# Where the weight blocks of the SwiGLU and projection products stand in SBUF: set in by 116 bytes instead of 112, even chunks ahead of odd ones with 128 bytes between

## The chip, the core and the metric

One core of a Trainium2 chip runs the whole program in one launch. The metric is the device time in microseconds (us). Before the change three runs gave 1672.34, 1673.3 and 1674.23 us; the median is 1673.3. A difference of about 0.2% (3.3 us) is what a measurement of this kernel can tell from no change.

## What is computed

One layer of a decoder, in fp32, for T = 576 tokens (a prompt of 512 and 8 sequences of 8 new tokens) of D = 1024 features:

```
h = modulate(rms_norm(x, n1_g), sh1, sc1)
x = x + 0.5 * g1 * (silu(h @ w1_gate) * (h @ w1_up)) @ w1_down          # D_FF = 2816
h = modulate(rms_norm(x, nm_g), sh2, sc2)
u, v, q, k, rv, rg, ga, gb = split(h @ w_in)                            # 10240 columns
o_a = gelu(u) * chunk_spatial_mix(layer_norm(gelu(v)))
o_b = head_rms(retention(rotary(q), rotary(k), rv)) * silu(rg)
x = x + g2 * (sigmoid(ga) * (o_a @ w_a) + sigmoid(gb) * (o_b @ w_b)) @ w_o
h = modulate(rms_norm(x, n2_g), sh3, sc3)
x = x + 0.5 * g3 * (silu(h @ w2_gate) * (h @ w2_up)) @ w2_down
y = rms_norm(x, final_g)
```

## The kernel before

**Products in three matmuls.** Every large product is made of fp32r matmuls. A weight and an activation are each split into a rounded part and a rest (hi and lo), and a product of 128 features is three matmuls into one PSUM bank: hi x hi, hi x lo, lo x hi. The stationary operand of a matmul is a block of 128x128 weights, the moving one a row of 288 tokens (H, half of T). `prod` (line 640) does this for 512 features, as four chunks of 128 features (j = 0..3), so it is 12 matmuls, all recorded at line 644. `proj` (line 472, matmuls at 478) does the same for the down projections and a few others.

**Two columns of blocks at a time.** FFN 1, FFN 2 and the projections q, k, rg, ga, gb of w_in go through `Plain`, `Pair` and their variants (from line 693 on). A `Pair` takes two blocks of 128 output columns over 1024 features. It makes the two outputs for both token halves by a seven-product scheme (sums of weight blocks such as `S`, `U`, `V` take the place of the eighth product), so it has seven calls of `prod`, 84 matmuls. The first two of each stage are `Plain`, with eight calls.

**The path of a weight.** `block_of` (676) loads one 512x128 block with one DMA on SP's queue into half of a raw tile (`wraw`). `put_hi` (657) rounds it on ACT into a tile `whl` (or, for one block alone, `whs`), `put_lo` (665) takes the rest on DVE into the same tile. ACT and DVE do this for the next pair while PE works on this one.

**Places.** `set_in` (144) makes a tile a little larger than its data and starts the data INTO = 28 words (112 bytes) in. Within a `whl` tile, hi and lo of two blocks follow each other, and each block is its four chunks of 128 words (512 bytes) one after another. The moving operand of chunk j is row j of a tile of [2, 4, 288] words, so these rows are 1152 bytes apart. 1152 is 4.5 times 256 and 512 is twice 256: modulo 256 bytes the distance from a moving row to its weight block moves by 128 from each chunk to the next. A `whl` tile is (2048 + 28) words, 8304 bytes, and the next of its four buffers starts 8320 bytes on, which is 32.5 times 256.

```
 144     def set_in(home, shape, room=INTO, **kw):
 149         t = home.tile([P, n + room], F32R, **kw)[:, INTO:INTO + n]
 642         for j in range(4):
 643             for z, (s, m) in enumerate(((wh, xh), (wh, xl), (wl, xh))):
 644                 PE.matmul(
 645                     ps[:, :H], lhsT=s[:, j * P:(j + 1) * P], rhs=m[:, j, :],
```

**Value products.** In `values_of` (matmuls at 1346 and 1359) and `values` (1576) it is the other way round: tokens are stationary, and 256 columns of a weight tile made by `load_w` move. Those tiles are set in by the same 112 bytes.

**Order.** PE's order is the order in which the code is written; at the three seams between stages it is a list of steps by name (BEGIN, INTO_MIX, INTO_FFN2). In the retention stage (about 750 to 1250 us) work lives in slots of 2304 bytes, of which there are NSLOT = 36, handed out in turn.

Of the kernel before, what the change touches and what calls it, by code (L numbers as in the profile page):

```python
# [8 lines left out]
F32 = mybir.dt.float32  # L9
F32R = mybir.dt.float32r  # L10
AF = mybir.ActivationFunctionType
ALU = mybir.AluOpType
# [3 lines left out]
P = 128  # L16
# [7 lines left out]
H = T // 2  # L24
# [3 lines left out]
DV = 256  # L28
EPS = 1e-6
NT = 5  # L30
SG = 4
NSLOT = 36
NSLOT2 = 12
SSLOT = 11
FSLOT = 12
GROUPS = (5, 6, 5, 6)

INTO = 28
HALF = (slice(0, H), slice(H, T))

BEGIN = """
# [40 lines left out]
def layer_kernel(ctx: ExitStack, tc: tile.TileContext, a):  # L82
    nc = tc.nc
    PE, DVE, ACT, POOL = nc.tensor, nc.vector, nc.scalar, nc.gpsimd
# [5 lines left out]
    wp = ctx.enter_context(tc.tile_pool(name="wp", bufs=1))  # L90
    places = ExitStack()
# [29 lines left out]
    now["sn"], now["whs"] = pool(places, "sn"), pool(places, "whs")  # L121

    def slot(shape, dt=F32):

# [37 lines left out]
    def whl(shape):  # L162
        small = len(shape) == 3 and shape[1] == 1
        tag = "whs" if small else "whl"
        return set_in(now["whs"] if small else wp, [P] + shape, tag=tag, name=nm(tag), bufs=1 if small else 4)
# [8 lines left out]
    def high_low(shape):  # L174
        t = whl([2] + shape)
        return t[:, 0], t[:, 1]

    def split_w(raw, eng=None):
        hi, lo = high_low(list(raw.shape[1:]))
        ACT.copy(out=hi, in_=raw)  # L180
        now["lo"] = (eng or DVE).tensor_tensor(out=lo, in0=raw, in1=hi.bitcast(F32), op=ALU.subtract)  # L181
        return hi, lo

    def load_w(src, k0, kc, c0, cols, eng=None):
        return split_w(load_raw(src, k0, kc, c0, cols), eng)

    def split(hi, lo, src):
        ACT.copy(out=hi, in_=src)  # L188
# [327 lines left out]
    class Operands:  # L516
# [123 lines left out]
    def prod(ps, w, x, fresh):  # L640
        (wh, wl), (xh, xl) = w, x
        for j in range(4):
            for z, (s, m) in enumerate(((wh, xh), (wh, xl), (wl, xh))):
                PE.matmul(  # L644
                    ps[:, :H], lhsT=s[:, j * P:(j + 1) * P], rhs=m[:, j, :],
                    start=fresh and j == 0 and z == 0, stop=j == 3 and z == 2, skip_group_check=True,
                )
        tick(cost(4))

    def snap(ps, t=None):  # L650
# [2 lines left out]
        ACT.copy(out=t, in_=ps[:, :H])  # L653
        return t

    class Weights:
        def put_hi(self, names, src, neg=False):
            hl = whl([2, len(names), 512])
            if neg:
                ACT.activation(out=hl[:, 0], in_=src, func=AF.Copy, scale=-1.0)  # L660
            else:
                ACT.copy(out=hl[:, 0], in_=src)  # L662
            self.hl[names] = hl, src, neg

        def put_lo(self, names):
            hl, src, neg = self.hl[names]
            if neg:
                now["lo"] = DVE.scalar_tensor_tensor(
                    out=hl[:, 1], in0=src, scalar=-1.0, in1=hl[:, 0].bitcast(F32), op0=ALU.mult, op1=ALU.subtract
                )  # L670
            else:
                now["lo"] = DVE.tensor_tensor(out=hl[:, 1], in0=src, in1=hl[:, 0].bitcast(F32), op=ALU.subtract)  # L672
            for i, m in enumerate(names):
                self.w[m] = (hl[:, 0, i], hl[:, 1, i])

        def block_of(self, dst, i, z):
# [16 lines left out]
    class Plain(Weights):  # L693


        def __init__(self, cols, n):
            self.cols, self.n, self.g, self.w, self.hl, self.raw = cols, n, None, {}, {}, []
            for z in range(2):
                t = raw4([2, 4, P])
                for i in range(2):  # L700
                    self.block_of(t[:, i], i, z)
                self.raw.append(t.rearrange("p m k c -> p m (k c)"))

        def nh(self):
            self.put_hi(("n11", "n21"), self.raw[0], True)
# [54 lines left out]
    class Pair(Weights):  # L760
        def __init__(self, cols):
            self.cols, self.w, self.hl = cols, {}, {}
            self.p, self.q = (raw4([2, 4, P]) for _ in range(2))
            for t, m, i, z in ((self.p, 0, 0, 0), (self.q, 1, 1, 0), (self.p, 1, 1, 1), (self.q, 0, 0, 1)):
                self.block_of(t[:, m], i, z)

            self.p, self.q = (t.rearrange("p m k c -> p m (k c)") for t in (self.p, self.q))

        def ah(self):
            self.put_hi(("a11", "a22"), self.p)  # L770
# [2 lines left out]
            self.put_lo(("a11", "a22"))  # L773

        def bh(self):
            self.put_hi(("a12",), self.q[:, 0:1])

        def bl(self):
            self.put_lo(("a12",))

        def S(self):
            DVE.tensor_tensor(out=self.p[:, 1], in0=self.q[:, 1], in1=self.p[:, 1], op=ALU.add)  # L782
            DVE.tensor_tensor(out=self.q[:, 1], in0=self.q[:, 1], in1=self.p[:, 0], op=ALU.add)  # L783

        def U(self):
            DVE.tensor_tensor(out=self.p[:, 0], in0=self.p[:, 1], in1=self.p[:, 0], op=ALU.add)  # L786

        def Sh(self):
            self.put_hi(("s2", "s1"), self.p)
# [2 lines left out]
            self.put_lo(("s2", "s1"))  # L792

        def V(self):
            DVE.tensor_tensor(out=self.q[:, 0], in0=self.p[:, 0], in1=self.q[:, 0], op=ALU.add)

        def Uh(self):
            self.put_hi(("s4", "s3"), self.q)
# [217 lines left out]
    parts = [First(0), First(1)]  # L1016
# [68 lines left out]
    for c in range(KC):  # L1085
# [34 lines left out]
    win = a["w_in"][0]  # L1120
# [433 lines left out]
    v = {}  # L1554
# [3 lines left out]
    I32 = mybir.dt.int32  # L1558

    def weights_v(i, z):  # L1560
        return [load_w(win, 4 * kk, 4, V0 + i * 512 + z * 256, 256) for kk in range(2)]

    def values(i, z, ws):

# [254 lines left out]
    for pr in ([0], [1], [2], [3], [4], [5], [6, 7]):  # L1819
# [4 lines left out]
        for h in range(2):  # L1824
            for c in pr:
                ps = proj(W[c], OA, h)
# [30 lines left out]
    now["xs1"], now["sn"], now["whs"] = pool(ffn2, "xs1"), pool(ffn2, "sn"), pool(ffn2, "whs")  # L1857
    now["wraw"] = pool(ffn2, "raw")
    ops.clear()
    now["hl"] = pool(hreg, "hl", "right")  # L1860
# [185 lines left out]
```

## Time and profile before

| | |
|---|---|
| median of 3 runs | 1673.3 us |
| the profiled execution's own time | 1672.59 us |
| its span, first to last instruction | 1670.8 us |
| PE busy | 1639.0 us, 98% |
| DVE, ACT, POOL busy | 69%, 47%, 17% |
| TensorE's granted clock, share of full speed | 0.997 |
| matmuls of line 644 | 5784 |
| matmuls of line 478 | 4032 |

Instructions on different engines overlap. Matmuls are pipelined, so a single matmul's record (295 ns) is much longer than the time from one matmul's start to the next; the latter is read from the starts and counts of the rows of the timeline. The record of a matmul and the spacing behind it rise and fall together.

### The profile page before, as it was taken

To read this page: it belongs to the slowest core of one execution; us is meant where nothing else is said; L and a number is where in the kernel's file an instruction comes from. 1 tells how busy PE (TensorE), PEld (TensorE's weight loads), DVE (VectorE), ACT (ScalarE), POOL (GpSimd) and SP (SyncE) were. 2 spreads that over 40 slices of the span, in tenths; PEclk is the share of its full clock that TensorE was granted. 3 is DMA by queue.
4 is the path that set the end of the run, shared out by engine and by line. 5 is a ranking of instruction groups with operands and counts; after the bars stand their busy time and mean duration, and the time that the engine had idled before them with its cause. 6 is when DMAs were issued, how large, how long until landed. Compare 5 with 4: busy or idle time off the path is not lost. (4 is left out here: it accounts for less than half of the span.)

```text
span 1670.8 us, 31364 instructions
## 1 busy us (share of the span) xinstructions
PE 1639.0 (98%) x12548; PEld 1576.0 (94%) x12548; DVE 1153.5 (69%) x1835; ACT 783.8 (47%) x1331; POOL 288.1 (17%) x372
## 2 busy tenths in 40 slices
PE   8999999999999999999999999999999999999997
PEld 4889999999999999999989999998999999999997
DVE  6867856576797777755697554676748868576773
ACT  5533524344564556544444454443236525343453
POOL 0000000000411111013245343454231000000002
PEclk9999999999999999999999999999999999999999
DMA  9443444332647676764457575799540333332331
GB/s 306 135 153 109 140 128 137 112 104 86 180 127 221 204 224 197 219 207 149 147 181 226 177 168 157 201 263 266 177 139 8 92 92 96 95 90 81 97 89 58
DMA packets 300212, 252.09 MB, mean 151 GB/s; under 512 B 13593, under 2 KB 260633, under 8 KB 300066
## 3 DMA queue, kind: packets, MB, share of 16 engines
q1 hardware_dynamic: 284594, 206.76, 40.9%
q0 software_dynamic: 13168, 40.97, 8.9%
q10 hardware_dynamic: 2304, 2.36, 0.4%
q8 instruction: 98, 1.61, 0.4%
q14 instruction: 48, 0.39, 0.1%
HBM read 207.01 MB, written 43.02 MB: 150 GB/s over the span
## 5 line engine op out<-in xcount | busy, mean ns | idle before, releaser
L644 PE MATMUL ps<-xa,whl 128*128 128x288 f32 x3000 | 422.4, 295 | 4.4 <-ACT whl L662 1.4
L644 PEld LDWEIGHTS ps<-xa,whl 128*128 128x128 f32 x3000 | 403.4, 190 | 17.3 <-issue 4.2
L644 PE MATMUL ps<-xs,whl 128*128 128x288 f32 x2040 | 289.2, 295 | 0.9 <-ACT sn L653 0.6
L644 PEld LDWEIGHTS ps<-xs,whl 128*128 128x128 f32 x2040 | 274.6, 189 | 11.0 <-issue 4.2
L672 DVE TENSOR_TENSOR whl<-wraw,whl 128x1024 fp32r<-128x1024 f32 x192 | 234.8, 1225 | 56.5 <-ACT whl L662 45.8
L662 ACT CAST whl<-wraw 128x1024 fp32r<-128x1024 f32 x192 | 200.4, 1049 | 111.2 <-DVE wraw L786 65.1
L478 PE MATMUL ps<-c,wd 128*128 128x288 f32 x1824 | 245.8, 295 | 0.0
L478 PEld LDWEIGHTS ps<-c,wd 128*128 128x128 f32 x1824 | 242.4, 188 | 3.5 <-issue 3.4
L478 PE MATMUL ps<-c,whl 128*128 128x288 f32 x1368 | 190.4, 297 | 1.1 <-ACT c L188 0.6
L478 PEld LDWEIGHTS ps<-c,whl 128*128 128x128 f32 x1368 | 182.8, 188 | 3.1 <-ACT c L188 1.1
L465 POOL TENSOR_TENSOR x<-x,s 128x64 f32<-128x64 f32 x72 | 34.8, 484 | 809.7 <-DVE s L464 782.4
L459 DVE SCALAR_TENSOR_TENSOR x<-ps,gate,x 128x288 f32<-128x288 f32 (+1 forms) x128 | 61.1, 481 | 117.2 <-PE ps L478 117.1
L653 ACT COPY sn<-ps 128x288 f32<-128x288 f32 x195 | 77.1, 398 | 104.3 <-PE ps L644 103.7
L181 DVE TENSOR_TENSOR whl<-wraw,whl 128x1024 fp32r<-128x1024 f32 x56 | 75.6, 1351 | 71.2 <-ACT whl L180 70.8
L945 ACT CAST wd<-wraw 128x640 fp32r<-128x640 f32 (+2 forms) x58 | 45.4, 783 | 106.2 <-PE ps L478 100.4
L1346 PE MATMUL ps<-whl,xx 128*128 128x256 f32 x768 | 91.5, 279 | 0.0
L1346 PEld LDWEIGHTS ps<-whl,xx 128*128 128x128 f32 x768 | 90.8, 188 | 0.0
L644 PE MATMUL ps<-xs,whs 128*128 128x288 f32 x480 | 69.7, 293 | 0.0
L180 ACT CAST whl<-wraw 128x1024 fp32r<-128x1024 f32 x56 | 58.5, 1049 | 22.7 <-PE ps L478 14.3
L644 PEld LDWEIGHTS ps<-xs,whs 128*128 128x128 f32 x480 | 65.5, 189 | 0.0
L662 ACT CAST whs<-wraw 128x512 fp32r<-128x512 f32 x62 | 38.4, 620 | 56.4 <-PE ps L644 46.6
L950 DVE TENSOR_TENSOR wd<-wraw,wd 128x640 fp32r<-128x640 f32 (+2 forms) x58 | 53.8, 928 | 9.9 <-ACT wd L945 9.9
(285 smaller groups left out, 2223.4 us busy)
## 6 DMA issues: line engine op xcount, KB each, us to landing
ada<-in_w_ada_dram SPq DMA_DIRECT2D x56, 512.0 KB
wraw<-in_w_in_dram SPq DMA_DIRECT2D x96, 256.0 KB
wraw<-in_w_gate_dram SPq DMA_DIRECT2D x88, 256.0 KB
wraw<-in_w_up_dram SPq DMA_DIRECT2D x88, 256.0 KB
wraw<-in_w_in_dram SPq DMA_DIRECT2D x32, 512.0 KB
wraw<-in_w_down_dram SPq DMA_DIRECT2D x32, 384.0 KB
wraw<-in_w_down_dram SPq DMA_DIRECT2D x32, 320.0 KB
accd<-c POOLq DMA_DIRECT2D x32, 288.0 KB, 5.8
```

The lines of the kernel that those rows point to most:

```text
L180: ACT.copy(out=hi, in_=raw)
L181: now["lo"] = (eng or DVE).tensor_tensor(out=lo, in0=raw, in1=hi.bitcast(F32), op=ALU.subtract)
L459: DVE.scalar_tensor_tensor(out=x[:, o:o + w], in0=ps[:, :w], scalar=g[:, c, 0:1], in1=x[:, o:o + w], op0=ALU.mult, op1=ALU.add)
L465: return lambda: POOL.tensor_tensor(out=x[:, NP:T], in0=x[:, NP:T], in1=u, op=ALU.add)
L478: PE.matmul(ps[:, :H], lhsT=s[:, k, c0:c0 + P], rhs=m[:, HALF[h]], start=k == 0 and z == 0, stop=k == kc - 1 and z == 2,)
L644: PE.matmul(ps[:, :H], lhsT=s[:, j * P:(j + 1) * P], rhs=m[:, j, :], start=fresh and j == 0 and z == 0, stop=j == 3 and z == 2, skip_group ...
L653: ACT.copy(out=t, in_=ps[:, :H])
L662: ACT.copy(out=hl[:, 0], in_=src)
L672: now["lo"] = DVE.tensor_tensor(out=hl[:, 1], in0=src, in1=hl[:, 0].bitcast(F32), op=ALU.subtract)
L945: ACT.copy(out=hl[:, 0], in_=self.raw[c])
L950: DVE.tensor_tensor(out=lo, in0=self.raw[c], in1=hi.bitcast(F32), op=ALU.subtract)
L1346: PE.matmul(ps[:, :DV], lhsT=s, rhs=m, start=i == 0, stop=i == 23)
```

## The change

It does five things.

1. The blocks of `prod` get a layout of their own (`block_w`): in a tile, first the even chunks (0 and 2) of all blocks, hi and then lo, starting BINTO = 29 words (116 bytes) in; then, after 32 free words (128 bytes), the odd chunks (1 and 3) in the same order. So modulo 256 an odd chunk's block stands 128 bytes further than an even chunk's.
2. The raw tiles get the same split, and `block_of` fills a block with two DMAs of 256x128 (even chunks, odd chunks) in place of one of 512x128.
3. ACT's rounding, DVE's rest and DVE's sums of weights read and write two runs in place of one, with the same count of elements and of instructions.
4. Weight tiles of `load_w` for the value products are set in by VINTO = 48 words (192 bytes) in place of 28.
5. A `whl` tile has 64 spare words in place of 28 (8448 bytes, 33 times 256, so that all four buffers start alike modulo 256); `whs` goes ahead of `sn` in memory; NSLOT falls from 36 to 35.

Set side by side by the addresses of the two builds: the distance from a moving row to the block of its own matmul, modulo 256, is 112 and 240 in turn from chunk to chunk before, and 116 in all chunks after. From the moving row to the block that the next matmul needs it is the same number for the first two matmuls of a chunk; for the third, whose next block is that of the next chunk, it is 244 after (before: as the chunk's own). For the value products, from moving row to stationary block, it is 16 or 144 before and 64 after.

```diff
-NSLOT = 36
+NSLOT = 35
 INTO = 28
+VINTO = 48
+BINTO = 29
...
-    def set_in(home, shape, room=INTO, **kw):
+    def set_in(home, shape, room=INTO, into=INTO, **kw):
...
-        t = home.tile([P, n + room], F32R, **kw)[:, INTO:INTO + n]
+        t = home.tile([P, n + room], F32R, **kw)[:, into:into + n]
...
+    def whl(shape, into=INTO):
+        return set_in(wp, [P] + shape, 64, into, tag="whl", name=nm("whl"), bufs=4)
...
-                    ps[:, :H], lhsT=s[:, j * P:(j + 1) * P], rhs=m[:, j, :],
+                    ps[:, :H], lhsT=s[j], rhs=m[:, j, :],
...
+    def block_w(n):
+        half = n * 2 * 2 * P
+        home, tag = (wp, "whl") if n == 2 else (now["whs"], "whs")
+        room = 2 * half + 64
+        t = home.tile([P, room], F32R, tag=tag, name=nm(tag), bufs=4 if n == 2 else 1)
+        parts = []
+        for z in range(2):
+            v = t[:, BINTO + z * n * 256:BINTO + z * n * 256 + 512 * n].rearrange("p (b r) -> p b r", b=2)
+            parts.append(bass.AP(v.tensor, v.offset, [v.ap[0], [half + 32, 2], v.ap[2]]))
+        return parts
...
         def put_hi(self, names, src, neg=False):
-            hl = whl([2, len(names), 512])
+            hl = block_w(len(names))
+            src = src.rearrange("p b m r -> p b (m r)")
...
             for i, m in enumerate(names):
-                self.w[m] = (hl[:, 0, i], hl[:, 1, i])
+                at = [slice(P * (2 * i + j // 2), P * (2 * i + j // 2 + 1)) for j in range(4)]
+                self.w[m] = [[w[:, j % 2, at[j]] for j in range(4)] for w in hl]
...
-            nc.sync.dma_start(
-                out=dst, in_=src[z * 4 * P:(z + 1) * 4 * P, c0:c0 + P].rearrange("(k p) c -> p k c", p=P)
-            )
+            src = src[z * 4 * P:(z + 1) * 4 * P, c0:c0 + P].rearrange("(a b p) c -> p b a c", p=P, b=2)
+            for b in range(2):
+                nc.sync.dma_start(out=t[:, b, m].rearrange("p (a c) -> p a c", c=P), in_=src[:, b])
...
-        wv = [load_w(win, 4 * i, 4, RV0 + hd * DV, DV) for i in range(2)]
+        wv = [load_w(win, 4 * i, 4, RV0 + hd * DV, DV, VINTO) for i in range(2)]
```

PE's and POOL's instructions keep their order and shapes throughout. DVE's and ACT's keep their order too; the subtractions and roundings of blocks have another shape. What is new is on SP's queue. Its opening, where the block loads of FFN 1 (`wraw`) stand between those of the first modulation weights (`xa`, `xs`), before:

```order
L356 DMA xa_165<-in_w_ada_dram 128x2x256 x4
L679 DMA wraw_170<-in_w_gate_dram 128x4x128
L679 DMA wraw_170<-in_w_up_dram 128x4x128
L679 DMA wraw_173<-in_w_gate_dram 128x4x128
L679 DMA wraw_173<-in_w_up_dram 128x4x128
L356 DMA xs_28_176<-in_w_ada_dram 128x2x256 x4
```

and of the change:

```order
L353 DMA xa_165<-in_w_ada_dram 128x2x256 x4
L697 DMA wraw_170<-in_w_gate_dram 128x2x128 x2
L697 DMA wraw_170<-in_w_up_dram 128x2x128 x2
L697 DMA wraw_175<-in_w_gate_dram 128x2x128 x2
L697 DMA wraw_175<-in_w_up_dram 128x2x128 x2
L353 DMA xs_28_180<-in_w_ada_dram 128x2x256 x4
```

Each load of a block has become two of half its size, ahead of the same `xs` loads. Across the program it is 272 block loads that become 544.

## Rows read from the trace of the kernel before

**Rows 1.** The page, part 1: busy time of each engine, its share of the span, instructions.

```profile
PE 1639.0 (98%) x12548; PEld 1576.0 (94%) x12548; DVE 1153.5 (69%) x1835; ACT 783.8 (47%) x1331; POOL 288.1 (17%) x372
```

**Rows 2.** Six stretches of 100 us: length, busy time and instructions of PE, of PE's weight loads, of DVE, ACT and POOL, then the granted clock, the DMA share and GB/s.

```profile
100.00:200.00 100.00, 100.00 (x758) 95.98 (x757) 69.82 (x117) 40.56 (x65) 3.64 (x8) 1.00 0.43 127
300.00:400.00 100.00, 99.77 (x755) 97.30 (x754) 73.33 (x120) 43.41 (x70) 3.09 (x8) 1.00 0.38 111
600.00:700.00 100.00, 100.00 (x757) 93.76 (x754) 76.50 (x114) 62.10 (x104) 10.80 (x20) 1.00 0.70 209
900.00:1000.00 100.00, 100.00 (x824) 97.57 (x824) 56.89 (x76) 45.89 (x82) 38.88 (x43) 1.00 0.60 169
1100.00:1200.00 100.00, 97.90 (x761) 94.33 (x760) 76.94 (x131) 37.94 (x72) 42.55 (x36) 1.00 0.87 259
1500.00:1600.00 100.00, 99.82 (x758) 99.59 (x757) 73.62 (x118) 44.31 (x70) 3.59 (x8) 1.00 0.32 94
```

**Rows 3.** Waits of PE: who waited for whom, us in total, times, longest.

```profile
PE ps L295 <- ACT ada L292: 4.4, 1, 4.4
PE ps L312 <- ACT ada L306: 3.6, 3, 2.0
...
PE ps L644 <- ACT whl L662: 1.4, 1, 1.4
PE ps L644 <- DVE whl L672: 1.3, 2, 0.8
```

**Rows 4.** Groups of PE's matmuls by line and tiles (out<-moving,stationary): count, busy time, mean ns of one record, idle time before them.

```profile
L644 PE MATMUL ps<-xa,whl 128*128 128x288 f32 x3000 | 422.4, 295 | 4.4 <-ACT whl L662 1.4 <-DVE whl L672 1.3 <-ACT xa L557 0.9
L644 PE MATMUL ps<-xs,whl 128*128 128x288 f32 x2040 | 289.2, 295 | 0.9 <-ACT sn L653 0.6
L644 PE MATMUL ps<-xs,whs 128*128 128x288 f32 x480 | 69.7, 293 | 0.0
L644 PE MATMUL ps<-xa,whs 128*128 128x288 f32 x264 | 38.8, 295 | 0.0
...
L1346 PE MATMUL ps<-whl,xx 128*128 128x256 f32 x768 | 91.5, 279 | 0.0
...
L1576 PE MATMUL ps<-whl,xx 128*128 128x256 f32 x384 | 47.9, 282 | 0.0
```

**Rows 5.** PE's timeline in FFN 1, from the end of a down projection (line 478) through two pairs: start, length from first start to last end, line, tiles, count.

```profile
336.86 12.14 PE L478 MATMUL ps<-c,wd 128*128 128x288 f32 x90
348.84 3.31 PE L644 MATMUL ps<-xs,whl 128*128 128x288 f32 x24
351.98 1.74 PE L644 MATMUL ps<-xa,whl 128*128 128x288 f32 x12
353.56 1.74 PE L644 MATMUL ps<-xs,whs 128*128 128x288 f32 x12
355.13 4.89 PE L644 MATMUL ps<-xa,whl 128*128 128x288 f32 x36
359.86 3.32 PE L644 MATMUL ps<-xs,whl 128*128 128x288 f32 x24
363.01 1.74 PE L644 MATMUL ps<-xa,whl 128*128 128x288 f32 x12
364.59 1.74 PE L644 MATMUL ps<-xs,whs 128*128 128x288 f32 x12
366.17 4.89 PE L644 MATMUL ps<-xa,whl 128*128 128x288 f32 x36
370.90 3.31 PE L644 MATMUL ps<-xs,whl 128*128 128x288 f32 x24
374.05 1.74 PE L644 MATMUL ps<-xa,whl 128*128 128x288 f32 x12
```

**Rows 6.** The first of those products at 348.84 us, chunk by chunk: PE's groups in stretches that hold the three matmuls of one chunk and no other, for chunk 0 (349.11 to 349.125 us), chunk 1 (349.50 to 349.52) and chunk 3 (350.29 to 350.305); the row of chunk 2 (349.89 to 349.91) reads as that of chunk 0. The number behind the comma is the mean ns of one record.

```profile
L644 PE MATMUL ps<-xs,whl 128*128 128x288 f32 x3 | 0.6, 295 | 0.0
L644 PE MATMUL ps<-xs,whl 128*128 128x288 f32 x3 | 0.6, 292 | 0.0
L644 PE MATMUL ps<-xs,whl 128*128 128x288 f32 x3 | 0.6, 291 | 0.0
```

**Rows 7.** PE's timeline in the retention stage, around one head's value products (1346, 1359).

```profile
950.39 11.40 PE L1346 MATMUL ps<-whl,xx 128*128 128x256 f32 x96
961.62 2.05 PE L1359 MATMUL ps<-whl,hs 128*128 128x256 f32 x16
963.51 1.76 PE L478 MATMUL ps<-c,whl 128*128 128x288 f32 x12
```

**Rows 8.** DVE's and ACT's groups for the blocks: count, busy time, mean ns of one, idle time before them and what ended it.

```profile
L672 DVE TENSOR_TENSOR whl<-wraw,whl 128x1024 fp32r<-128x1024 f32 x192 | 234.8, 1225 | 56.5 <-ACT whl L662 45.8 <-DMA wraw<-in_w_in_dram 5.2 <-DMA ada<-in_w_ada_dram 1.6
...
L662 ACT CAST whl<-wraw 128x1024 fp32r<-128x1024 f32 x192 | 200.4, 1049 | 111.2 <-DVE wraw L786 65.1 <-PE ps L644 33.7 <-DMA wraw<-in_w_up_dram 7.1
```

**Rows 9.** SP's timeline in the opening (start, length, queue, line, tiles, count) and PE's wait there.

```profile
18.82 0.37 SPq L679 DMA_DIRECT2D wraw<-in_w_gate_dram  x1
19.57 0.37 SPq L679 DMA_DIRECT2D wraw<-in_w_up_dram  x1
20.31 0.81 SPq L679 DMA_DIRECT2D wraw<-in_w_gate_dram  x1
21.16 1.28 SPq L679 DMA_DIRECT2D wraw<-in_w_up_dram  x1
22.48 5.58 SPq L356 DMA_DIRECT2D xs<-in_w_ada_dram  x8
...
31.32 4.07 PE L300 MATMUL ps<-xs,cs 128*32 128x512 f32 x10 [0.34 <-DMA xs<-in_w_ada_dram]
```

More of the change, by code (lines that the diff above doesn't have):

```diff
@@ L120, in layer_kernel @@
     now["xa"], now["xs1"] = pool(places, "xa"), pool(places, "xs1")
-    now["sn"], now["whs"] = pool(places, "sn"), pool(places, "whs")
+    now["whs"], now["sn"] = pool(places, "whs"), pool(places, "sn")
     def slot(shape, dt=F32):
@@ L160, in raw4 @@
         )
[L162 to L165, printed above, removed]
+    def whl(shape, into=INTO):
+        return set_in(wp, [P] + shape, 64, into, tag="whl", name=nm("whl"), bufs=4)
     def load_raw(src, k0, kc, c0, cols):
@@ L172, in load_raw, with split_w, load_w @@
         return raw
[L174 to L179, printed above, removed]
+    def split_w(raw, into=INTO):
+        t = whl([2] + list(raw.shape[1:]), into)
+        hi, lo = t[:, 0], t[:, 1]
         ACT.copy(out=hi, in_=raw)
-        now["lo"] = (eng or DVE).tensor_tensor(out=lo, in0=raw, in1=hi.bitcast(F32), op=ALU.subtract)
+        now["lo"] = DVE.tensor_tensor(out=lo, in0=raw, in1=hi.bitcast(F32), op=ALU.subtract)
         return hi, lo
-    def load_w(src, k0, kc, c0, cols, eng=None):
-        return split_w(load_raw(src, k0, kc, c0, cols), eng)
+    def load_w(src, k0, kc, c0, cols, into=INTO):
+        return split_w(load_raw(src, k0, kc, c0, cols), into)
     def split(hi, lo, src):
@@ L654, in snap, with blocks @@
         return t
+    def block_w(n):
[8 more added lines that the diff above has]
+        return parts
     class Weights:
+        def blocks(self):
+            return raw4([2, 2, 2, P]).rearrange("p b m a c -> p b m (a c)")
         def put_hi(self, names, src, neg=False):
-            hl = whl([2, len(names), 512])
+            hl = block_w(len(names))
+            src = src.rearrange("p b m r -> p b (m r)")
             if neg:
-                ACT.activation(out=hl[:, 0], in_=src, func=AF.Copy, scale=-1.0)
+                ACT.activation(out=hl[0], in_=src, func=AF.Copy, scale=-1.0)
             else:
-                ACT.copy(out=hl[:, 0], in_=src)
+                ACT.copy(out=hl[0], in_=src)
             self.hl[names] = hl, src, neg
@@ L668, in put_lo, with block_of @@
                 now["lo"] = DVE.scalar_tensor_tensor(
-                    out=hl[:, 1], in0=src, scalar=-1.0, in1=hl[:, 0].bitcast(F32), op0=ALU.mult, op1=ALU.subtract
+                    out=hl[1], in0=src, scalar=-1.0, in1=hl[0].bitcast(F32), op0=ALU.mult, op1=ALU.subtract
                 )
             else:
-                now["lo"] = DVE.tensor_tensor(out=hl[:, 1], in0=src, in1=hl[:, 0].bitcast(F32), op=ALU.subtract)
+                now["lo"] = DVE.tensor_tensor(out=hl[1], in0=src, in1=hl[0].bitcast(F32), op=ALU.subtract)
             for i, m in enumerate(names):
-                self.w[m] = (hl[:, 0, i], hl[:, 1, i])
-        def block_of(self, dst, i, z):
+                at = [slice(P * (2 * i + j // 2), P * (2 * i + j // 2 + 1)) for j in range(4)]
+                self.w[m] = [[w[:, j % 2, at[j]] for j in range(4)] for w in hl]
+        def block_of(self, t, m, i, z):
             src, c0 = self.cols[i]
-            nc.sync.dma_start(
-                out=dst, in_=src[z * 4 * P:(z + 1) * 4 * P, c0:c0 + P].rearrange("(k p) c -> p k c", p=P)
-            )
+            src = src[z * 4 * P:(z + 1) * 4 * P, c0:c0 + P].rearrange("(a b p) c -> p b a c", p=P, b=2)
+            for b in range(2):
+                nc.sync.dma_start(out=t[:, b, m].rearrange("p (a c) -> p a c", c=P), in_=src[:, b])
         def finish_hi(self):
@@ L698, in __init__ @@
             for z in range(2):
-                t = raw4([2, 4, P])
+                t = self.blocks()
                 for i in range(2):
-                    self.block_of(t[:, i], i, z)
-                self.raw.append(t.rearrange("p m k c -> p m (k c)"))
+                    self.block_of(t, i, i, z)
+                self.raw.append(t)
         def nh(self):
@@ L762, in __init__ @@
             self.cols, self.w, self.hl = cols, {}, {}
-            self.p, self.q = (raw4([2, 4, P]) for _ in range(2))
+            self.p, self.q = self.blocks(), self.blocks()
             for t, m, i, z in ((self.p, 0, 0, 0), (self.q, 1, 1, 0), (self.p, 1, 1, 1), (self.q, 0, 0, 1)):
-                self.block_of(t[:, m], i, z)
-            self.p, self.q = (t.rearrange("p m k c -> p m (k c)") for t in (self.p, self.q))
+                self.block_of(t, m, i, z)
         def ah(self):
@@ L775, in bh @@
         def bh(self):
-            self.put_hi(("a12",), self.q[:, 0:1])
+            self.put_hi(("a12",), self.q[:, :, 0:1])
         def bl(self):
@@ L781, in S @@
         def S(self):
-            DVE.tensor_tensor(out=self.p[:, 1], in0=self.q[:, 1], in1=self.p[:, 1], op=ALU.add)
-            DVE.tensor_tensor(out=self.q[:, 1], in0=self.q[:, 1], in1=self.p[:, 0], op=ALU.add)
+            DVE.tensor_tensor(out=self.p[:, :, 1], in0=self.q[:, :, 1], in1=self.p[:, :, 1], op=ALU.add)
+            DVE.tensor_tensor(out=self.q[:, :, 1], in0=self.q[:, :, 1], in1=self.p[:, :, 0], op=ALU.add)
         def U(self):
-            DVE.tensor_tensor(out=self.p[:, 0], in0=self.p[:, 1], in1=self.p[:, 0], op=ALU.add)
+            DVE.tensor_tensor(out=self.p[:, :, 0], in0=self.p[:, :, 1], in1=self.p[:, :, 0], op=ALU.add)
         def Sh(self):
@@ L794, in V @@
         def V(self):
-            DVE.tensor_tensor(out=self.q[:, 0], in0=self.p[:, 0], in1=self.q[:, 0], op=ALU.add)
+            DVE.tensor_tensor(out=self.q[:, :, 0], in0=self.p[:, :, 0], in1=self.q[:, :, 0], op=ALU.add)
         def Uh(self):
@@ L1560, in weights_v @@
     def weights_v(i, z):
-        return [load_w(win, 4 * kk, 4, V0 + i * 512 + z * 256, 256) for kk in range(2)]
+        return [load_w(win, 4 * kk, 4, V0 + i * 512 + z * 256, 256, VINTO) for kk in range(2)]
     def values(i, z, ws):
@@ L1856, in layer_kernel @@
     xs = [xt2[c // 2][:, c % 2] for c in range(KC)]
-    now["xs1"], now["sn"], now["whs"] = pool(ffn2, "xs1"), pool(ffn2, "sn"), pool(ffn2, "whs")
+    now["xs1"], now["whs"], now["sn"] = pool(ffn2, "xs1"), pool(ffn2, "whs"), pool(ffn2, "sn")
     now["wraw"] = pool(ffn2, "raw")
```

## The prediction

> **What bounds the kernel now.** I read the page's busy times first: PE is busy 98% of the span, DVE 69%, ACT 47% [rows 1]. The stretches of 100 us say that this holds nearly everywhere: 97.9 to 100 us of each are PE's, at the full granted clock [rows 2]. PE's waits are small. The longest at the start is 4.4 us, and the matmuls of `prod` waited 1.4 us in all for ACT's rounding of blocks and 1.3 us for DVE's rest [rows 3]. So the end is set by how many matmuls there are and how far apart they start, and the change alters neither their number nor their order. What is left is the spacing.
>
> The spacing is read from starts, since records overlap. From 348.84 to 374.05 us PE starts 24+12+12+36+24+12+12+36+24 = 192 matmuls of `prod` in 25.21 us: 131.3 ns each [rows 5]. At 2.4 GHz, the level that the clock of 1.00 in these stretches [rows 2] stands for, a row of 288 tokens is 120 ns if each token takes one cycle; the matmuls of 256 columns, at 117.0 ns [rows 7], fit that (14.3 ns less for 32 columns, 13.3 by the cycle). So 11.3 ns of each are something else. 3000+2040+480+264 = 5784 matmuls [rows 4] at 131.3 ns are 759 us, 45% of the span, and the 11.3 ns are 65 us of it.
>
> Then one product of four chunks taken apart [rows 6]: the records of chunks 0 and 2 average 295 ns, those of 1 and 3 292 and 291. All twelve have the same shapes, stand in one tile and come without a wait. What alternates from chunk to chunk is where the weight block stands relative to the moving row: modulo 256 bytes, 240 in chunks 0 and 2 here, 112 in chunks 1 and 3. So the trace before already shows that place costs time: 295 - 291.5 = 3.5 ns a matmul. Around the mean of 131.3 that makes about 129.5 ns for a chunk at 112 and 133.1 for one at 240 (an estimate, for records and spacing need not move one to one). A second row supports the dear value: in `proj` before 348.84 us, whose distance stays the same through one token half, 90 matmuls take 11.98 us, 133.1 ns each [rows 5].
>
> **The change part by part.**
>
> *Blocks of prod.* All chunks now stand at 116 for their own matmul, 4 bytes from the cheap 112. But while a matmul runs, PE already loads the next weights, and there a third of the matmuls differ: the third of each chunk has the next chunk's block before it, at 244, 4 bytes from the dear 240. No row has an operand set in by an odd multiple of 4 bytes, so what 116 itself does must be bounded. If every matmul goes like a chunk at 112, the gain is 1.8 x 5784 = 10 us. If every one goes like a chunk at 240, the loss is 10 us. The nearest rows are those of chunks at 112, for two matmuls of three; for the third I take neither end but today's mean. (129.5 + 129.5 + 131.3) / 3 = 130.1 ns, 1.2 ns less than now: **-7 us**. With the third at 133.1 it would be 130.7 ns and -3 us, so -3 to -10 is this term's own range. Below it, the floor is the 120 ns of the columns, -65 us, which no row comes near.
>
> *Value products.* 768 and 384 matmuls of 256 columns [rows 4], and a few more for the new tokens, now have distance 64 where they had 16 or 144. 96 of them take 11.23 us, 117.0 ns, and 16 take 1.89 us, 118.1 ns, against 106.7 ns for the columns [rows 7]: the same excess of 10 to 11 ns at both distances. Nothing says which way 64 goes. 0 us, with 1.8 ns either way as above: 1152 x 1.8 = 2 us, both ends kept.
>
> *Block loads.* 272 DMAs become 544 of half the size, with the same 512-byte runs. An issue takes SP 0.37 us when the queue is free [rows 9], so a pair's four extra issues are 1.5 us of SP in the 11 us that a pair takes PE. Behind them in line are the loads of the next pair; ACT waited only 7.1 us in all for those blocks [rows 8]. So that is hidden. In the opening it isn't quite: four extra issues, 4 x 0.37 = 1.5 us, stand ahead of the `xs` loads for which PE waits 0.34 us at 31.32 [rows 9]. The older four took 3.66 us of SP (18.82 to 22.48), 0.81 and 1.28 us where the queue held them up, so part of the extra is not felt: **+1 us**, 0 to +2.
>
> *Two runs in place of one* on ACT and DVE: same elements, same count. 1049 ns and 1225 ns [rows 8] may grow by a little. Both engines have room (DVE 73 to 77%, ACT 38 to 62% in the stretches of [rows 2]), and PE's 2.7 us of waits for them [rows 3] say that blocks are ready in time. 0 us; were each of the 192 subtractions 100 ns longer, that is 19 us of DVE spread over stages where it idles a quarter of the time.
>
> *One slot less, and whs ahead of sn.* In the retention stage a slot is handed out again one turn earlier. PE is full there but for 2 us in 1100 to 1200 [rows 2]. 0 us, up to +3 if a reader of the slot is late.
>
> Sum: 1672.6 of the profiled execution (0.7 under the median of 1673.3) - 7 + 1 = 1666.6; against the median, **1667 us**.
>
> **A rule against it.** What [rows 6] show is that two chunks alike in all but place differ by 3.5 ns. The Trainium skill, TensorE: Matmul & The Clock Gate, in its step-by-step on what happens when a matmul is issued, says that PE has two independent read ports on SBUF and that loading the next weights takes nothing from the running matmul. By that rule the place can't matter, and this change would give 0 in place of -7. The same page puts the spacing of warm matmuls at the columns' time and about 2.5 ns, 122.5 ns here by an estimate; the 131.3 ns of [rows 5] don't agree.
>
> **Rivals.**
>
> *A, no change.* The difference of [rows 6] is not the distance but goes with the order (the first matmuls of a chunk pay for what the chunk before left behind), so that cheap and dear places only trade. For it: the means of `prod` (131.3) and of `proj` at a fixed distance (133.1) lie close, though one alternates and the other doesn't [rows 5]. Against: chunk 3 repeats chunk 1. Then PE's spacing stays within 0.3 ns, 2 us, and with the opening's +1 the time is about 1674. The rule above gives the same time.
>
> *B, slower.* A block that starts 116 bytes in no longer starts on a multiple of 16 bytes, and a fixed distance keeps every chunk in one pattern: if that is the dear one, as in `proj` at 133.1 ns [rows 5], each of the 5784 pays 1.8 ns more. +10 us, and with the opening and the value products' bad end 1686. It decides as soon as the mean of `prod` is over 131.9 ns (+3.3 us). For it: the one row with a fixed distance is the dear one, and the third matmul's 244. Against: two matmuls of three lie nearest the cheap row.
>
> *C, a larger gain.* Two of three matmuls lose half of the 11.3 ns: 2/3 x 5784 x 5.65 = 22 us, 1651. For it: the excess differs with place at all, and 112 need not be the best place. Against: no chunk in the trace is under some 129 ns.
>
> **Chances.** Forecast (-3 to -10 us) 0.36, A 0.22, B 0.25, C 0.17. About 0.2% (3.3 us) is what a measurement can tell from no change. Faster: most of the forecast (0.32), all of C, some of A's spread (0.03): 0.52. Within 0.2%: 0.04 of the forecast, most of A, a little of B: 0.23. Slower: 0.25. As cases of both signs count, the range goes from C's time with the value products' good end (1649) to B's (1686), less a microsecond or so at each end for what 2 in 10 leave out: 1649 to 1685. The forecast's own range is 1663 to 1671.
>
> **What would show it.** Right: the starts in an FFN stretch put `prod` at about 130 ns; the four chunks of a product have records of equal mean; `proj` keeps 133 ns; the page's waits of PE on blocks stay near 3 us; SP's opening shows eight issues in place of four and the `xs` matmuls start up to 2 us later. Wrong: `prod` still at 131.3 (A), above it (B), below 128 (C); waits of PE on ACT, DVE or block loads that add up to more than 5 us (then the hidden parts were not hidden); or value products that moved by more than 2 ns.

## The result, and the profile after

| | kernel before | changed kernel |
|---|---|---|
| median | 1674.24 us (20 runs, 1670.77 to 1677.35) | 1676.33 us (20 runs, 1671.70 to 1678.32) |
| ratio | | 1.0014, 95% interval 1.0008 to 1.0021 |
| profiled execution (its span) | 1672.59 us (1670.8) | 1671.70 us (1669.9) |

The changed kernel is 2.1 us slower (1.3 to 3.5 by the interval). That is under the 0.2% that a measurement can tell from no change. The forecast was 1667 us. The profiled execution of the changed kernel is the fastest of its 20, so the terms are read from spacings and waits, not from the difference of the two spans.

What PE does is as before [rows 1, 2, 4]: the page's part 1, then one stretch of 100 us and two groups of matmuls (columns as there).

```profile
PE 1636.9 (98%) x12548; PEld 1575.2 (94%) x12548; DVE 1156.7 (69%) x1835; ACT 783.7 (47%) x1331; POOL 288.3 (17%) x372
```

```profile
300.00:400.00 100.00, 99.86 (x752) 97.39 (x752) 73.31 (x120) 42.40 (x68) 3.09 (x8) 1.00 0.40 111
```

```profile
L641 PE MATMUL ps<-xa,whl 128*128 128x288 f32 x3000 | 424.0, 297 | 4.4 <-ACT whl L677 1.4 <-DVE whl L687 1.3 <-ACT xa L554 1.0
...
L1361 PE MATMUL ps<-whl,xx 128*128 128x256 f32 x768 | 89.1, 277 | 0.0
```

The engine is as full and the clock as high. The mean record of `prod` went from 295 to 297 ns and that of the value products from 279 to 277: two small shifts of opposite sign. The starts say how large they are. PE's timeline in FFN 1, the same 192 matmuls as in [rows 5] (24+12+12+36+24+12+12+36+24; the rows between the first and the last are left out):

```profile
347.87 3.34 PE L641 MATMUL ps<-xs,whl 128*128 128x288 f32 x24
...
373.26 1.75 PE L641 MATMUL ps<-xa,whl 128*128 128x288 f32 x12
```

25.39 us for 192, 132.2 ns each, where they took 25.21, 131.3 ns. Over 5784 matmuls that is **+5.4 us**. (Over the whole of the two traces, spacings above 150 ns left out, the means are 131.4 and 132.3 ns.) The same look at the value products [rows 7]:

```profile
949.58 11.06 PE L1361 MATMUL ps<-whl,xx 128*128 128x256 f32 x96
960.48 1.98 PE L1374 MATMUL ps<-whl,hs 128*128 128x256 f32 x16
962.29 1.75 PE L475 MATMUL ps<-c,whl 128*128 128x288 f32 x12
```

10.90 us for 96, 113.5 ns each, where they took 117.0. From start to start, all 1344 value products (with those of the new tokens) took 161.9 us in the trace before and take 157.9 now: **-4.0 us**.

The first product at 347.87 us, chunk by chunk as in [rows 6], stretches that hold one chunk's three matmuls (chunk 0, then chunk 1; chunk 2 reads as chunk 1, chunk 3 as chunk 0):

```profile
L641 PE MATMUL ps<-xs,whl 128*128 128x288 f32 x3 | 0.6, 295 | 0.0
L641 PE MATMUL ps<-xs,whl 128*128 128x288 f32 x3 | 0.6, 296 | 0.0
```

The four chunks are now nearly alike, but at the level of the dear chunks of before (295), not of the cheap ones (292 and 291). Matmul by matmul they are not alike, though every chunk has the same distances. From 349.46 us on the starts are 130, 140, 127, 133, 130, 134, 131, 132 and 133 ns apart, and then the same again: the pattern returns after three chunks, where a product has four. In the whole trace 93% of `prod`'s spacings return within 1 ns after nine matmuls, 34% after three. So a matmul's spacing hangs on what ran before it too, and not on its places alone.

Last, PE's waits, which answer to [rows 3]. First three rows of the kernel before that were not shown there, then the changed kernel's:

```profile
PE ps L1376 <- POOL c L1324: 1.9, 2, 1.0
...
PE ps L478 <- ACT c L188: 0.6, 1, 0.6
...
PE ps L478 <- DVE c L189: 0.5, 1, 0.5
```

```profile
PE ps L309 <- ACT ada L303: 4.3, 3, 2.0
...
PE ps L1391 <- POOL c L1339: 2.4, 2, 1.5
...
PE ps L641 <- ACT whl L677: 1.4, 1, 1.4
PE ps L641 <- DVE whl L687: 1.3, 2, 0.8
PE ps L475 <- DVE c L1843: 1.2, 1, 1.2
```

The waits for blocks are the same 2.7 us. All of PE's waits in this view add up to 24.0 us before and 25.6 after, **+1.6 us**. The rows that grew most are two of the retention stage (POOL's and DVE's `c`, by 0.5 and 0.7 us) and the wait for `ada` (by 0.7, 3.6 in [rows 3]). So 5.4 - 4.0 + 1.6 = 3.0 us, where the medians differ by 2.1.

### The profile page after: what moved, and what is told of

Read it like the earlier page. It is cut to its first block, busy times and chain, and to the rows that moved or that the text cites. A ratio compares the mean times of both kernels' runs of the same rounds, so it can differ in the third digit from the quotient of the medians.

```text
span 1669.9 us, 31828 instructions
## 1 busy us (share of the span) xinstructions
PE 1636.9 (98%) x12548; PEld 1575.2 (94%) x12548; DVE 1156.7 (69%) x1835; ACT 783.7 (47%) x1331; POOL 288.3 (17%) x372
## 4 chain that ended last, share of the span: by engine, by line
PE 88%; DMA 4%; DVE 4%; ACT 1%; POOL 1%; issue 1%; SPq 1%; POOLq 0%; ACTq 0%; DVEq 0%
PE ps L641 44%; PE ps L475 29%; PE ps L1361 4%; PE ps L297 2%; PE ps L1591 2%; PE ps L1453 1%; DMA wraw<-in_w_in_dram 1%; DMA xa<-in_w_ada_dram 1%; PE ps L1491 1%; PE ps L1374 1%; DMA c<-accd 1%; PE ps L1497 1%; PE ps L1469 0%; DVE whl L687 0%; DMA wraw<-in_w_down_dram 0%
## 5 line engine op out<-in xcount | busy, mean ns | idle before, releaser
L687 DVE TENSOR_TENSOR whl<-wraw,whl 128x1024 fp32r<-128x1024 f32 x192 | 235.3, 1227 | 53.0 <-ACT whl L677 45.0
L677 ACT CAST whl<-wraw 128x1024 fp32r<-128x1024 f32 x192 | 200.8, 1051 | 105.8 <-DVE wraw L801 60.4
```

Of the source, the lines that this page charges most:

```text
L677: ACT.copy(out=hl[0], in_=src)
L687: now["lo"] = DVE.tensor_tensor(out=hl[1], in0=src, in1=hl[0].bitcast(F32), op=ALU.subtract)
```

## Experiments

Each starts from the changed kernel unless it says otherwise. "Spacing" is that of the 192 matmuls from the first `prod` row to the last one shown. The spacings of single products and matmuls are worked out from the starts in the traces, their places from the addresses of the builds. Numbers 3 to 8 and 11 ran once each, for the trace; their times are no comparison. The granted clock is 1.00 in 347 to 375 us of every trace.

**1. The values alone.** The kernel before with `VINTO = 48`, the longer `whl` tiles and one slot less that this needs; blocks of `prod` as before.

```diff
...
-        return [load_w(win, 4 * kk, 4, V0 + i * 512 + z * 256, 256) for kk in range(2)]
+        return [load_w(win, 4 * kk, 4, V0 + i * 512 + z * 256, 256, VINTO) for kk in range(2)]
...
-        wv = [load_w(win, 4 * i, 4, RV0 + hd * DV, DV) for i in range(2)]
+        wv = [load_w(win, 4 * i, 4, RV0 + hd * DV, DV, VINTO) for i in range(2)]
```

> The kernel before with one part of the change: only the weights of the value products are set in by 192 bytes (48 elements, distance 64 between the moving row and the weights), all blocks of prod stay as they were (112 and 240 by turns). If the value products' cheaper spacing in the kernel after is their own distance, they go at 113.9 to 114.8 ns here too, where they had 117.0 to 117.9, prod stays at 131.3 to 131.4 ns, and the time is 1344 x 3.3 ns = 4.3 us under the kernel before. Rival: the value products gained from what the blocks around them do (other chunks at a fixed distance); then they stay at 117 ns and the time is that of the kernel before within 1 us.

```profile
348.96 3.31 PE L645 MATMUL ps<-xs,whl 128*128 128x288 f32 x24
...
374.16 1.74 PE L645 MATMUL ps<-xa,whl 128*128 128x288 f32 x12
...
951.01 11.06 PE L1347 MATMUL ps<-whl,xx 128*128 128x256 f32 x96
961.90 1.98 PE L1360 MATMUL ps<-whl,hs 128*128 128x256 f32 x16
```

`prod` at 25.20 / 192 = 131.3 ns, values at 10.89 / 96 = 113.4 ns. Time 1670.79 us against 1673.94, ratio 0.9983 (0.9974 to 0.9992): -3 us, with -4.3 inside the interval. The values' gain is their own. PE's waits add up to 25.2 us, 1.2 more than before, with the same 1.2 us for DVE's `c`: this part of the +1.6 comes with the values and the slots, not with the blocks.

**2. The blocks alone.** `VINTO = 28` in place of 48, which sets the value products at a constant 144.

> The kernel after without its value part: blocks of prod as in the change (116, even chunks ahead of odd ones, 128 bytes between), the weights of the value products back at 112 bytes in. If the blocks are what costs, prod stays at 132.3 ns and the time is 5784 x 0.96 ns = 5.5 us over the kernel before (value products at 117 ns), 1 to 2 us less if a constant distance of 144 suits the value products. Rival, that prod's higher spacing is the work of the set-in values or of the opening: prod falls back to 131.4 ns, and the time is that of the kernel before within 1.5 us.

```profile
350.56 3.34 PE L641 MATMUL ps<-xs,whl 128*128 128x288 f32 x24
...
375.95 1.75 PE L641 MATMUL ps<-xa,whl 128*128 128x288 f32 x12
...
953.82 11.12 PE L1361 MATMUL ps<-whl,xx 128*128 128x256 f32 x96
964.78 1.98 PE L1374 MATMUL ps<-whl,hs 128*128 128x256 f32 x16
```

`prod` stays at 132.2 ns, as expected. Values at 10.96 / 96 = 114.2 ns: at a constant 144 they gain nearly what they gain at 64, more than the "1 to 2 us" allowed for. So the time, 1674.94 us, ratio 1.0008 (0.9999 to 1.0017), is near the changed kernel's and not 5.5 us up.

**3. 112 in place of 116** (`BINTO = 28`), and **4. no 128 bytes between** (`[half, 2]` for `[half + 32, 2]`).

> The kernel after with the blocks of prod set in by 112 bytes in place of 116, all else alike: own distance 112 in every chunk, the third matmul of a chunk loads the next block at 240. This is the forecast's own case without the odd 4 bytes. Theory that 116 costs because it is no multiple of 16: prod falls to (133 + 127 + 135) / 3 = 131.7 ns or less, down to the forecast's 130.1. Theory that a fixed pattern of two loads at one distance and one at the other costs, whatever the 4 bytes: prod stays at 132.0 to 132.4 ns. Theory of cheap and dear places that only trade: 131.3 ns.

> The kernel after without the 128 bytes between the even and the odd chunks: the distances then go 116 and 244 by turns, chunk by chunk, as 112 and 240 did in the kernel before. Theory that the 4 bytes cost: prod stays near 132.3 ns. Theory that the pattern (each third matmul at the other distance) costs: prod falls back to 131.3 to 131.4 ns, 5.5 us of PE less than in the kernel after.

Number 3:

```profile
347.45 3.31 PE L641 MATMUL ps<-xs,whl 128*128 128x288 f32 x24
...
372.62 1.74 PE L641 MATMUL ps<-xa,whl 128*128 128x288 f32 x12
```

Number 4:

```profile
349.68 3.33 PE L641 MATMUL ps<-xs,whl 128*128 128x288 f32 x24
...
375.06 1.75 PE L641 MATMUL ps<-xa,whl 128*128 128x288 f32 x12
```

131.1 and 132.2 ns. The four bytes cost 1.1 ns in the same layout, and without the gap, with places going by turns as before, 116 and 244 still cost 132.2. So the layout in even and odd chunks is not what costs. And 112 in every chunk (with 240 as the third matmul's next), the forecast's own case without the odd 4 bytes, is hardly better than 112 and 240 by turns (131.3).

**5. Blocks at 64, values at 16** (`BINTO = 16`, `VINTO = 60`), **6. blocks at 0, values off 16** (`BINTO = 0`, `VINTO = 49`), **7. blocks at 120** (`BINTO = 30`).

> The kernel after with two places changed, both multiples of 16 bytes. Blocks of prod are set in by 64 bytes in place of 116 (own distance 64, the third matmul's next block at 192); the weights of the value products by 240 bytes, distance 16 throughout. Blocks, theory that only a start off 16 bytes costs and the distance hardly counts: prod at 131.0 to 131.4 ns, as at 112. Theory that 64 is a cheap distance in itself, as the value products' gain at 64 would have it: prod falls by the same 3.3 ns, to 128 ns, some 19 us less than the kernel before. Values, theory that the kernel before lost there by the distance going 16 and 144 by turns: 113.4 to 114 ns at a constant 16. Theory that 16 is the dear distance (the mean of 16 and 144 was 117.2 and 144 alone gave 113.8): 120.6 ns.

> The kernel after with blocks of prod set in by 0 bytes (distance 0, the third's next at 128; a multiple of 16), and the weights of the value products by 196 bytes in place of 192 (4 bytes off a multiple of 16, distance 68). Theory of the odd 4 bytes: prod at 131.0 to 131.4 ns, and the value products, which have 116's fault now, rise from 113.4 or 114 by about 1 ns to 114.5 to 115. Theory of distances: prod moves with 0 (weights and moving row alike in their low address bits; over 133 if they meet in the same place), the value products stay within 0.3 ns, since 64 and 68 are neighbours.

> The kernel after with blocks of prod set in by 120 bytes in place of 116: a multiple of 8 bytes, not of 16. Theory that a block off a multiple of 16 bytes reaches into one more piece of each row, however far off: prod at 132.2 to 132.4 ns, as at 116. Theory that only starts off 8 bytes cost: 131.1 to 131.3 ns, as at 112.

(In number 6 the values' distance is 60, not 68: here the set-in weights are the moving side.) Number 5:

```profile
351.93 3.36 PE L641 MATMUL ps<-xs,whl 128*128 128x288 f32 x24
...
377.52 0.70 PE L641 MATMUL ps<-xa,whl 128*128 128x288 f32 x4
...
959.42 11.41 PE L1361 MATMUL ps<-whl,xx 128*128 128x256 f32 x96
970.66 2.04 PE L1374 MATMUL ps<-whl,hs 128*128 128x256 f32 x16
```

Number 6:

```profile
348.73 3.36 PE L641 MATMUL ps<-xs,whl 128*128 128x288 f32 x24
...
374.26 1.76 PE L641 MATMUL ps<-xa,whl 128*128 128x288 f32 x12
...
958.88 11.68 PE L1361 MATMUL ps<-whl,xx 128*128 128x256 f32 x96
970.39 2.08 PE L1374 MATMUL ps<-whl,hs 128*128 128x256 f32 x16
```

Number 7:

```profile
349.91 3.37 PE L641 MATMUL ps<-xs,whl 128*128 128x288 f32 x24
...
375.58 1.76 PE L641 MATMUL ps<-xa,whl 128*128 128x288 f32 x12
```

Blocks: 133.3 ns at 64, 133.0 at 0, 133.7 at 120. Both theories of number 5 fail: 64 is a multiple of 16 and dear, and it is not cheap for `prod` though it is for the values. 120 is dearer than 116, which "one more piece of each row" doesn't give. What is left is that each place has a mean of its own. Values: 117.1 ns at a constant 16, 119.9 at 60. There too both theories of number 5 fail: a constant 16 costs what 16 and 144 by turns cost (117.0), and 144 alone costs 114.2.

**8. All places in one run.** Each pair takes another place; tiles are 128 bytes longer.

```diff
...
-        room = 2 * half + 64
+        room = 2 * half + 96
+        into = 23 * now.setdefault("blocks", 0) % 64
+        now["blocks"] += 1
...
```

> The kernel after in which each pair of blocks of prod takes another place: set in by 0 to 252 bytes in steps of 4 (23 x the pair's number, modulo 64 elements), so that all 64 distances modulo 256 occur, each in 36 to 168 matmuls; and each value weight another set-in, 24 distances. Theory that starts off 16 bytes cost: the spacing by distance is a comb, low at multiples of 16 and about 1 ns or more higher between. Theory that every distance has a price of its own (112: 131.2, 116: 132.3, 120: 133.7, 64: 133.3, 0: 132.9 so far): a smooth or stepped curve over the distance in which neighbours are alike and multiples of 16 don't stand out; if it repeats after 128 bytes, 112 and 240 cost the same and the alternation in the kernel before did nothing. A cheap place below 130 ns, if there is one, shows here; the unweighted mean over all places would be 132.5 to 133 ns, and the whole run 7 to 9 us over the kernel before.

Spacing within the products, by distance of the own block (423 products; 3 to 11 each):

```
cheapest:  244 130.1   192 131.2   240 131.3   112 131.4   252 131.5
dearest:   180 134.4    68 134.3    84 134.1   132 134.1    52 134.0
tried:     112 131.4   116 132.5   120 133.9    64 133.0     0 132.5
16 multiples of 16: mean 132.4 (131.2 to 133.7)
48 others:          mean 132.7 (130.1 to 134.4)
```

There is no comb: the cheapest place, 244, is 4 bytes off a multiple of 16. Neighbours are not alike either (244 and 248 are 130.1 and 132.8), nor are places 128 apart (116 and 244). The correlation over the pairs is under 0.2 in both cases. The five places tried alone agree with the scan within 0.5 ns. So the second theory holds in its main part, that each place has a mean of its own, but its smooth curve doesn't. The time was 1679.56 us against 1675.8, 4 us more, not 7 to 9 (one run each).

**9. Blocks at 244** (`BINTO = 61`, tiles 128 bytes longer), **10. the same with chunks in the order 0, 2, 1, 3**, **11. this order alone** (`BINTO = 29`).

```diff
-        for j in range(4):
+        for j in (0, 2, 1, 3):
```

> The kernel after with blocks of prod set in by 244 bytes in place of 116, the cheapest of the 64 places of the scan (130.1 ns), where the third matmul of each chunk has the next block at 116. Theory that every distance has a price of its own: prod at 130.1 to 130.5 ns, 5784 x 1.0 to 1.2 = 6 to 7 us less than the kernel before, and with the value products' 4.3 us about 1663 to 1665 against 1674. Theory that the price hangs on the start modulo 16 (244 is 4 over a multiple of 16, as 116): 132.3 ns as in the kernel after, no difference from it.

> The same with the chunks of a product taken in the order 0, 2, 1, 3, so that the next block stands at the distance of the own one except at two of twelve matmuls (after chunk 2, and where the product ends). If the place of the next block counts as much as that of the own one, prod falls below what it has in order 0, 1, 2, 3; with 116 at every third matmul that would have been (2 x 130.1 + 132.3) / 3 = 130.8, and here 130.1 to 130.4 ns. If the next block's place counts for nothing, both are alike within 0.2 ns.

> The kernel after with the chunks of a product taken in the order 0, 2, 1, 3 and nothing else: now ten matmuls of twelve have the next block at 116 too, where it was two of three. If the third matmuls' 244 is what costs in the kernel after (the dear part of the forecast's term), prod falls from 132.3 ns to about 131.5 or less. If 116 has its own price, as in the scan (132.3 ns where own and next are both 116), it stays at 132.2 to 132.4 ns.

Numbers 9 and 10 didn't do what they were for. A tile longer by 128 bytes shifts every second buffer, so 3264 matmuls had 244 and 2520 had 116, and the values 64 and 192 by turns (115.8 and 117.7 ns). Times: 1675.23 us, ratio 1.0009 (1.0000 to 1.0018), and 1678.17, ratio 1.0023 (1.0013 to 1.0033), against 1674.01. Their products still tell something, taken by place: at 244, 130.65 ns in number 9 and 131.8 in number 10; at 116, 132.3 and 132.8. Number 11:

```profile
349.23 3.36 PE L641 MATMUL ps<-xs,whl 128*128 128x288 f32 x24
...
374.82 1.76 PE L641 MATMUL ps<-xa,whl 128*128 128x288 f32 x12
```

133.3 ns where the changed kernel has 132.2. With 116 for own and next block in ten matmuls of twelve it is 1.1 ns dearer. The third matmul's 244 was not what costs; it helps. Neither theory had that.

**12. Odd chunks ahead of even ones**, all else as in the change: every own distance is 244, the third's next block at 116.

```diff
-                self.w[m] = [[w[:, j % 2, at[j]] for j in range(4)] for w in hl]
+                self.w[m] = [[w[:, 1 - j % 2, at[j]] for j in range(4)] for w in hl]
...
-                nc.sync.dma_start(out=t[:, b, m].rearrange("p (a c) -> p a c", c=P), in_=src[:, b])
+                nc.sync.dma_start(out=t[:, 1 - b, m].rearrange("p (a c) -> p a c", c=P), in_=src[:, b])
```

> The kernel after with one thing turned round: in each place the odd chunks stand ahead of the even ones, all else alike (116 bytes in, 128 between, values at 192). So every own distance is 244 in place of 116, and the third matmul's next block stands at 116 in place of 244. In the kernel that was to try this before, whose buffers fell on 116 and on 244 by turns because its tiles grew by 128 bytes each, the products at 244 ran at 130.0 ns in 133, 127, 130 over and over (130.65 over all 238 of them), those at 116 at 132.3. Theory that every pair of own and next distance has a price of its own: prod at 130.0 to 130.7 ns, 4 to 8 us under the kernel before, values at 113.4 to 114.0 ns for 4.3 us more: 1662 to 1666 against 1674. Theory that starts 4 bytes off a multiple of 16 cost: 132.3 ns, no difference from the kernel after. Theory that the turns of 116 and 244 helped there: above 130.7 here.

```profile
347.28 3.29 PE L641 MATMUL ps<-xs,whl 128*128 128x288 f32 x24
...
372.24 1.72 PE L641 MATMUL ps<-xa,whl 128*128 128x288 f32 x12
```

24.96 us for 192, 130.0 ns, in 133, 127, 130 over and over. Time 1668.08 us against 1673.47, ratio 0.9966 (0.9952 to 0.9979): 5.4 us faster (3.5 to 8.0), the best kernel of this study. The spacings give more: -7.5 us of `prod` and -4.2 of values are -11.7. PE's waits took some of it back. They add up to 29.2 us, 5.2 more than before; these grew most:

```profile
PE ps L1391 <- POOL c L1339: 2.9, 2, 1.6
...
PE ps L641 <- ACT sn L650: 1.9, 6, 0.4
...
PE ps L297 <- DMA xs<-in_w_ada_dram: 1.5, 2, 1.1
```

1.0, 1.3 and 1.2 us more than the 1.9, 0.6 and 0.3 of before. A faster PE may come to some of its inputs early; that is not shown, and the last row stands at 0.8 in number 1 too. That leaves -6.5 us, inside the interval.

## Why the prediction was wrong

**The step that failed is the term of the blocks.** "The nearest rows are those of chunks at 112, for two matmuls of three": -7 us forecast, +5.4 measured. By the matmul's position in a chunk (mean ns from its start to the next one, whole traces, spacings above 150 ns left out):

| own distance, the third's next | first (hi x hi) | second (hi x lo) | third (lo x hi) | mean |
|---|---|---|---|---|
| before, chunks at 112, 112 | 131.9 | 127.2 | 131.5 | 130.2 |
| before, chunks at 240, 240 | 131.1 | 133.1 | 133.4 | 132.6 |
| number 3: 112, 240 | 132.5 | 127.4 | 133.7 | 131.2 |
| changed kernel: 116, 244 | 131.5 | 134.3 | 131.1 | 132.3 |
| number 12: 244, 116 | 133.2 | 127.0 | 130.1 | 130.1 |

The first two rows bear out the estimate of 129.5 and 133.1 ns for the chunks of before. The term then failed twice.

- *The third matmul was put too low.* It was taken at 131.3 ns. In number 3, the forecast's own case without the odd 4 bytes, the first two matmuls of a chunk average 130.0 ns, near the 129.5 forecast for them, but the third takes 133.7. That leaves 131.1 to 131.2 ns, a gain of some 0.2 where 1.2 was forecast.
- *116 doesn't go like 112.* "4 bytes from the cheap 112" was taken as near. In number 3 against the changed kernel, 4 bytes are 1.1 ns: the second matmul goes from 127.4 to 134.3, the third back from 133.7 to 131.1. In the scan neighbours are hardly more alike than any two places.

The forecast's 130.1 ns and 0.3 for the first two, 0.8 for the third and 1.1 for the 4 bytes are 132.3.

**A row that was misread.** The 133.1 ns of `proj` before 348.84 us were to support the dear value. They hold one spacing of 217 ns, without which the mean is 132.2, and by the addresses half of the matmuls stand at 112 (132.0 ns) and half at 240 (132.3). In the whole trace before, `proj` on `wd` with own and next block at 112 takes 132.0 ns (874 matmuls), at 240 132.5 (872), and the same after the change. So the trace before had 112 kept up over many matmuls, and there it was not cheap.

**Rival A** had the time about right and not the cause. By it the first matmuls of a chunk pay, but in the chunks of before the second and third differ. What holds of it is that a chunk's spacing doesn't go with its place alone: 112 has 130.2 ns in `prod` by turns and 132.0 in `proj`, and 244 has 132.7 by turns with 116 (number 4) and 130.1 in number 12.

The text had seen that "no row has an operand set in by an odd multiple of 4 bytes" and bounded the term by 10 us either way. That bound held the +5.4; the choice within it did not. At 116 the third matmul, whose next block was counted as half a loss, is a gain beside the rest (131.1 of a mean of 132.3; number 11).

**Rival B** set its point at a mean of `prod` over 131.9 ns. It came to 132.2, so B's side was taken for the blocks, with half its price. Its cause isn't the one: a start off a multiple of 16 bytes is neither dear as such (244, 130.0 ns) nor are multiples safe (64, 133.3).

**The value products** were sized 0, with 2 us either way, because 16 and 144 seemed to cost the same excess. They gave -4.0 us, beyond the bound. The row of 117.0 ns was that of both places by turns (117.4 ns at 16, 117.1 at 144, so the reading was right), and 144 alone is cheaper by 2.8 ns (number 2). This is why the time came out within 0.2%, as in rival A, for another reason and by luck: two terms that nearly cancel.

**The rule that spoke against the change.** The Trainium skill, TensorE: Matmul & The Clock Gate, in its step-by-step, has the weights' loading take nothing from a running matmul. The time near no change agrees with it only by accident: places alone moved `prod` from 130.0 to 133.7 ns in runs that differ in nothing else of PE's work, so as far as the rule has the place not matter, the measurement decides against it here. That it is the loading that takes from the matmul is not shown.

**Small terms.** SP's opening, which answers to [rows 9]:

```profile
19.95 1.12 SPq L697 DMA_DIRECT2D wraw<-in_w_gate_dram  x2
21.46 1.14 SPq L697 DMA_DIRECT2D wraw<-in_w_up_dram  x2
22.96 1.12 SPq L697 DMA_DIRECT2D wraw<-in_w_gate_dram  x2
24.46 1.15 SPq L697 DMA_DIRECT2D wraw<-in_w_up_dram  x2
25.72 4.78 SPq L353 DMA_DIRECT2D xs<-in_w_ada_dram  x8
```

Eight issues, as forecast, and the `xs` loads issue 3.2 us later. FFN 1's first `prod` matmul starts at 36.03 us, where it was 35.32: 0.7 us later, inside the 0 to +2. But in number 1, whose block loads are those of before, it starts at 36.44, so these runs don't show that the loads are the cause. DVE's subtraction and ACT's rounding, [rows 8], keep their length:

```profile
L687 DVE TENSOR_TENSOR whl<-wraw,whl 128x1024 fp32r<-128x1024 f32 x192 | 235.3, 1227 | 53.0 <-ACT whl L677 45.0 <-DMA wraw<-in_w_in_dram 4.1 <-DMA wraw<-in_w_up_dram 0.6
L677 ACT CAST whl<-wraw 128x1024 fp32r<-128x1024 f32 x192 | 200.8, 1051 | 105.8 <-DVE wraw L801 60.4 <-PE ps L641 29.9 <-DMA wraw<-in_w_up_dram 9.9
```

1227 and 1051 ns where they were 1225 and 1049. The slot less may be the 0.7 us more that PE waits for DVE's `c`, inside the 0 to +3; number 1 has one slot less and faster values together, so which of them it is stays open.

**What stays open.** Why a place has its price. The runs rule out a simple rule by 16 bytes, by a repeat after 128, by nearness, by the own block alone, or by own and next place together (the pattern of nine, and 112 and 244 above); they don't show what meets in memory.

## What to carry over

Where PE is full and no wait ends its idle time, compare start-to-start spacings at each operand place. When a place is said to be cheap, measure it alone and in the order in which it will run, because a difference between neighbours in a pattern need not be a price that moves with them. Look for that place in other rows of the trace at hand too: `proj` held 112 for whole token halves. Where places have no law that one can argue from, put many of them into one kernel and read the spacing by place: one run of that found 244, which no argument had pointed to.

## What the runs showed of the hardware

- A matmul of 288 columns starts every 130.0 to 133.7 ns (means of 192, granted clock 1.00), by the place of its weight block against its moving row, with nothing else of PE's work changed; one of 256 columns every 113.4 to 119.9 ns. 4 bytes can cost 1.1 ns (112 to 116) or 6 (64 to 60, values).
- The same place has not always the same spacing. In the changed kernel the places repeat after three matmuls and the spacings after nine, from 127 to 140 ns. Value products at 144 take 117.1 ns by turns with 16 and 114.2 alone; `prod` at 244 takes 132.7 by turns with 116 (number 4) and 130.1 where all own blocks are at 244 (number 12).
- The order of a product's chunks, with the same own places, costs 1.1 ns a matmul (132.2 to 133.3, number 11).
- The place of a buffer depends on the length of its pool's tiles: 128 bytes more in each turned one distance into two (numbers 9 and 10).
